# Layer 1's MLP products with the high and low parts of the activations as one 512-column operand, and layer 0's MLP in 256-column blocks with three matmuls

## The chip, the cores and the metric

The kernel runs on one core of a Trainium2 chip. The metric is the time of one execution in device microseconds (us). The engines are TensorE (PE: matmuls, and the weight loads PEld in front of them), VectorE (DVE), ScalarE (ACT), GpSimd (POOL) and SyncE (SP), which issues the weight DMAs.

## The reference

Two layers over 256 tokens with a model width of 2048 and a hidden width of 8192. The mixer (three kinds of token mixing between one input and one output projection) is not touched. The part that matters is the MLP of each layer, in fp32:

```python
mod = (cond @ ada_w[layer] + ada_b[layer])[:, None, :]
sh_a, sc_a, g_a, sh_m, sc_m, g_m = jnp.split(mod, N_MOD, axis=-1)
...
x = x + g_a * hybrid_mixer(...)
h = rmsnorm(x, norm_mlp_w[layer]) * (1.0 + sc_m) + sh_m
x = x + g_m * (jnp.square(jax.nn.relu(h @ w_ff1[layer])) @ w_ff2[layer])
...
return rmsnorm(x, final_norm_w)
```

## The kernel before

Activations lie transposed: 16 tiles of 128 features (k = 0 to 15) by T = 256 tokens. Every fp32 operand is split into a high part (rounded to fp32r) and a low part (what is left), and each product is three matmuls into the same sum: high weights by low activations, low weights by high activations, high by high. In `mm_b` (L252 to L254) the weights are the stationary 128x128 tile and the 256 token columns stream, four output tiles n to one k. In `mm_a` (L263 to L265), used for some input projections, the activations are stationary and 512 weight columns stream.

Weights arrive as `raw` pieces of 512 KB (2 k by 512 columns), six buffers. `split` makes of each the high part `wh` on ACT (L221, 128x1024) and the low part `wl` (L227) on DVE or, for the share `pool_share` of the pieces, on POOL; both have three buffers. A piece feeds 24 matmuls of `mm_b` (2 k, 4 n, three each). The share is 0.8 in layer 0's MLP and 0 in layer 1's.

In the MLP, `ff1` makes a block of 512 hidden features (16 k), and squares its ReLU into a high and a low tile of 128x1024 each (`square`: ACT L964 ReLU out of PSUM, L969 square, L971 high, DVE L972 low). There are 16 such blocks. `ff2` takes two of them (a step s) and adds to the residual X, in four output blocks nb of 512 features; the residual update is four DVE instructions of 128x256 per block, out of PSUM (`residual`, L796). Sums lie in two PSUM pairs `pj` of 1024 columns; the next block but one needs the pair again. Layer 1 does ff1 in one group of 16 k, layer 0 does its first 6 blocks in two groups of 8 k.

The normalised activations h are made by `h_make` in pairs of k: X times R (DVE L492), scale and shift (ACT L497, twice), high part (ACT L499), low part (DVE L500). R is the norm's factor: a sum of squares `ss` (DVE L374, L375), summed over features on PE (L383), DVE's Newton steps, and back over PE and ACT (L401, R copied by ACT L405). To have work for PE meanwhile, `lead` starts the next stage's first block on unnormalised activations (258 columns, L471 to L473; its operand is made ahead by `lead_u`, DVE L437 with L432 and L433, called by `early` out of the stage before), and `lead_out` puts R in afterwards (ACT L484, DVE L485). At the end of the program `ff2_tail` does the last 512 output features in four cuts of 128 (L1012 to L1014, residual L1017), with the sums of squares between.

The adaptive scale and shift vectors (`ada`, DVE L283, weights on their own DMAs) are computed piecemeal between these steps until the middle of layer 1. The order on each engine isn't written by hand: a scheduler at build time orders the instructions of every engine, so that an edit moves others.

Of the kernel before, what the change touches and what calls it, by code (L numbers as in the profile page):

```python
# [62 lines left out]
class Trunk:  # L63
# [166 lines left out]
    def chunk(self, src, nk, ncol=512):  # L230
# [11 lines left out]
        return out  # L242

# [204 lines left out]
    def lead(self, l, js, jc, wsrc, kts, stat_at):  # L448
# [5 lines left out]
        for c, k0 in enumerate(range(kts[0], kts[-1] + 1, 4)):  # L454
# [5 lines left out]
            w = self.chunk(wsrc(k0, nk), nk)  # L460
            if js == 3:
                self.step(nk / 4)
            for k in range(k0, k0 + nk):
                if k not in self.U:
                    self.lead_u(l, js, jc, [k, k + 1])
                (wh, wl), (uh, ul) = w[k - k0], self.U.pop(k)
                f, e = k == kts[0], k == kts[-1]
                for n in range(4):
                    s = slice(n * P, n * P + P)
                    o = ps[n][:, :LT]  # L470
                    nc.tensor.matmul(o, lhsT=wh[:, s], rhs=ul, start=f, stop=False)  # L471
                    nc.tensor.matmul(o, lhsT=wl[:, s], rhs=uh, start=False, stop=False)
                    nc.tensor.matmul(o, lhsT=wh[:, s], rhs=uh, start=False, stop=e)  # L473
# [4 lines left out]
        return ps  # L478

# [8 lines left out]
    def h_make(self, l, js, jc, kts, psum=False):  # L488
        nc = self.nc
        for k in kts[::2]:  # L490
# [8 lines left out]
            nc.scalar.copy(self.hh[:, k:k + 2, :], t)  # L499
            nc.vector.tensor_tensor(self.hl[:, k:k + 2, :], t, self.hh[:, k:k + 2, :].bitcast(F32), ALU.subtract)  # L500

    def hact(self, k):
        return self.hh[:, k, :], self.hl[:, k, :]
# [330 lines left out]
    def layer(self, l):  # L834
# [6 lines left out]
        for g, kts in enumerate(G):  # L841
            self.pump_until(l, 0, kts[-1])
            led = g == 0 and cfg["lead_win"]
            if led:
                ps = self.lead(l, 0, 1, lambda k, n: io["w_in"][l, 0, k // 4][:, k % 4:k % 4 + n, :], kts, cfg["stat_win"])
# [62 lines left out]
        for g, kts in enumerate(G):  # L908
# [4 lines left out]
            if led:  # L913
                ps = self.lead(l, 3, 4, lambda k, n: io["w_ff1"][l, 0, k // 4][:, k % 4:k % 4 + n, :], kts, cfg["stat_ff1"])
            self.h_make(l, 3, 4, kts)
            if led:
                acc[0] = self.slot()
                if kts[-1] == KT - 1:
                    self.lead_out(ps, acc[0], AF.Relu)
                    acc[0] = self.square(acc[0])  # L920
                else:
                    self.lead_out(ps, acc[0])
# [15 lines left out]
    def ff1(self, l, b, kts, acc=None):  # L938
        nc = self.nc
        ps = self.pair()  # L940
        for k0 in range(kts[0], kts[-1] + 1, 4):
            nk = min(4, kts[-1] + 1 - k0)
            r0 = k0 % 4
            w = self.chunk(self.io["w_ff1"][l, b, k0 // 4][:, r0:r0 + nk, :], nk)
            for i in range(nk):
                k = k0 + i
                self.mm_b(ps, w[i], self.hact(k), k == kts[0], k == kts[-1])
            self.step(nk / 4)
        if kts[-1] != KT - 1:
            if acc is None:  # L950
                acc = self.slot()
                nc.scalar.copy(self.flat(acc), ps)
            else:
                d = self.flat(acc)
                nc.vector.tensor_tensor(d, ps, d, ALU.add)
            return acc
        if acc is not None:
            t = acc
            d = self.flat(t)
            nc.vector.tensor_tensor(d, ps, d, ALU.add)  # L960
            nc.scalar.activation(t, t, AF.Relu)
        else:
            t = self.slot()
            nc.scalar.activation(self.flat(t), ps, AF.Relu)  # L964
        return self.square(t)

    def square(self, t):
        nc = self.nc
        nc.scalar.activation(t, t, AF.Square)  # L969
# [178 lines left out]
```

## Time and profile before

| | before |
|---|---|
| time of the runs | 2549.27 us median of 3 (2548.29 to 2551.44) |
| profiled execution | 2549.75 us, span of its trace 2548.0 us, mean granted TensorE clock 0.977 of full speed |
| PE busy | 2450.1 us (96% of the span) |
| DVE, ACT, POOL busy | 1583.2, 1180.9, 758.9 us |
| DMA | 630.45 MB, 247 GB/s over the span |

The profiled execution took 1.7 us more than its span, and 0.5 us more than the median of the runs. The stages in the trace: layer 0's MLP lies at about 540 to 1310 us, layer 1's at about 1800 to the end. PE is busy nearly throughout, so the trace is read for how far apart its matmuls stand and for the few places where it waits.

### The profile page before, as it was taken

Reading aid. Unit: us, or ns where it says so; the run is one execution under the profiler, and the core shown is the slowest. Engines: PE = TensorE matmul, PEld = TensorE weight load, DVE = VectorE, ACT = ScalarE, POOL = GpSimd, SP = SyncE. Lnnn points to the kernel's source line nnn. Section 1 sums busy time; section 2 is a strip of 40 time slices with the busy share of each in tenths; the row PEclk is TensorE's granted clock in tenths of the full one; section 3 lists DMA queues with packets and bytes.
Section 4 is the critical chain, followed back from the end, with each engine's and each line's share of the span. In section 5 each row is a group of like instructions: output and inputs, shape, how many; then the busy total and the mean of one; then the engine's idle time right before and its main releaser. Section 6 shows DMA issues by size and latency. Waiting matters only on the chain.

```text
span 2548.0 us, 46455 instructions
## 1 busy us (share of the span) xinstructions
PE 2450.1 (96%) x19016; PEld 2378.3 (93%) x19016; DVE 1583.2 (62%) x2427; ACT 1180.9 (46%) x1442; POOL 758.9 (30%) x314
## 2 busy tenths in 40 slices
PE   7999998979999999999989999999999999999997
PEld 6899977979999999999988989899999999999997
DVE  5867878788655444444478777656754555555554
ACT  4444455535544444444446446454644444344443
POOL 4786531212676766767650000000000000000000
PEclk8999999989999999999989999999999999999998
DMA  9899867788998888888867777555555555555552
GB/s 359 299 327 329 305 217 265 285 299 338 322 334 310 279 288 297 287 280 298 285 213 241 272 247 266 192 166 178 178 182 186 188 182 183 187 185 183 186 187 91
DMA packets 177246, 630.45 MB, mean 247 GB/s; under 512 B 19588, under 2 KB 24326, under 8 KB 177032
## 3 DMA queue, kind: packets, MB, share of 16 engines
q1 hardware_dynamic: 176600, 627.08, 70.8%
q8 instruction: 149, 2.44, 0.4%
q14 instruction: 65, 0.53, 0.1%
q10 hardware_dynamic: 432, 0.39, 0.1%
HBM read 625.30 MB, written 2.10 MB: 246 GB/s over the span
## 4 chain that ended last, share of the span: by engine, by line
PE 79%; DVE 9%; DMA 4%; issue 3%; POOL 3%; ACT 2%; SPq 0%; DVEq 0%; POOLq 0%; ACTq 0%
PE pj L253 23%; PE pj L252 23%; PE pj L254 23%; DMA ada<-ada_w 3%; POOL wl L227 3%; DVE ada L283 2%; PE pj L264 2%; PE pj L265 2%; PE pj L263 2%; DVE wl L227 2%; PE mx L620 1%; ACT wh L221 1%; DVE cv L709 1%; DVE blk L437 0%; DMA raw<-ada_w 0%
## 5 line engine op out<-in xcount | busy, mean ns | idle before, releaser
L221 ACT CAST wh<-raw 128x1024 fp32r<-128x1024 f32 x804 | 840.4, 1047 | 1129.8 <-PE pj L254 881.3
L227 POOL TENSOR_TENSOR wl<-raw,wh 128x1024 fp32r<-128x1024 f32 (+1 forms) x309 | 756.3, 2451 | 583.4 <-ACT wh L221 565.3
L227 DVE TENSOR_TENSOR wl<-raw,wh 128x1024 fp32r<-128x1024 f32 x495 | 615.7, 1246 | 487.4 <-ACT wh L221 486.7
L252 PE MATMUL pj<-hl,wh 128*128 128x256 f32 x2912 | 830.9, 286 | 9.5 <-DVE hl L500 8.2
L253 PE MATMUL pj<-hh,wl 128*128 128x256 f32 x2912 | 830.4, 285 | 7.2 <-DVE wl L227 7.2
L254 PE MATMUL pj<-hh,wh 128*128 128x256 f32 x2912 | 828.1, 284 | 0.0
L253 PE MATMUL pj<-blk,wl 128*128 128x256 f32 x2528 | 713.6, 282 | 6.6 <-DVE wl L227 5.2
L252 PE MATMUL pj<-blk,wh 128*128 128x256 f32 x2528 | 712.8, 282 | 2.8 <-ACT blk L538 1.5
L254 PE MATMUL pj<-blk,wh 128*128 128x256 f32 x2528 | 711.3, 281 | 0.0
L283 DVE SCALAR_TENSOR_TENSOR ada<-ada,cond 128x1024 f32<-128x1024 f32 x380 | 456.7, 1214 | 227.7 <-DMA ada<-ada_w 225.6
L252 PEld LDWEIGHTS pj<-hl,wh 128*128 128x128 f32 x2912 | 561.8, 193 | 10.7 <-DVE hl L500 8.9
L253 PEld LDWEIGHTS pj<-hh,wl 128*128 128x128 f32 x2912 | 562.4, 193 | 9.3 <-DVE wl L227 8.7
L254 PEld LDWEIGHTS pj<-hh,wh 128*128 128x128 f32 x2912 | 562.1, 193 | 0.2
L253 PEld LDWEIGHTS pj<-blk,wl 128*128 128x128 f32 x2528 | 478.5, 189 | 7.3 <-DVE wl L227 5.6
L252 PEld LDWEIGHTS pj<-blk,wh 128*128 128x128 f32 x2528 | 478.8, 190 | 3.4 <-ACT blk L538 1.9
L254 PEld LDWEIGHTS pj<-blk,wh 128*128 128x128 f32 x2528 | 479.3, 190 | 0.0
L1045 POOL TENSOR_TENSOR blk<-blk,R 128x1024 f32<-128x1024 f32 x1 | 2.4, 2357 | 1199.1 <-ACT R L405 1199.1
L264 PE MATMUL pj<-wl,hh 128*128 128x512 f32 x384 | 155.4, 405 | 8.5 <-DVE wl L227 8.4
L796 DVE SCALAR_TENSOR_TENSOR X<-pj,mod,X 128x256 f32<-128x256 f32 x284 | 117.8, 477 | 64.0 <-PE pj L254 63.9
L263 PE MATMUL pj<-wh,hl 128*128 128x512 f32 x384 | 153.2, 399 | 1.2 <-ACT wh L221 1.2
L265 PE MATMUL pj<-wh,hh 128*128 128x512 f32 x384 | 152.9, 398 | 0.0
L264 PEld LDWEIGHTS pj<-wl,hh 128*128 128x128 f32 x384 | 73.7, 192 | 24.5 <-DVE wl L227 10.7
(232 smaller groups left out, 1648.0 us busy)
## 6 DMA issues: line engine op xcount, KB each, us to landing
raw<-w_ff SPq DMA_DIRECT2D x508, 512.0 KB, 4.1
ada<-ada_w SPq DMA_DIRECT2D x380, 512.0 KB, 6.3
raw<-w_in SPq DMA_DIRECT2D x224, 512.0 KB, 5.0
raw<-w_out SPq DMA_DIRECT2D x64, 512.0 KB, 4.4
X<-x SPq DMA_DIRECT2D x4, 512.0 KB, 6.2
raw<-ada_w SPq DMA_DIRECT2D x4, 512.0 KB, 10.0
raw<-w_ff SPq DMA_DIRECT2D x8, 256.0 KB, 3.4
out<-blk SPq DMA_DIRECT2D x4, 512.0 KB, 2.8
```

The lines of the kernel that those rows point to most:

```text
L221: nc.scalar.copy(hi, raw)
L227: eng.tensor_tensor(lo, raw, hi.bitcast(F32), ALU.subtract)
L252: nc.tensor.matmul(o, lhsT=wh[:, s], rhs=al, start=st, stop=False, skip_group_check=True)
L253: nc.tensor.matmul(o, lhsT=wl[:, s], rhs=ah, start=False, stop=False, skip_group_check=True)
L254: nc.tensor.matmul(o, lhsT=wh[:, s], rhs=ah, start=False, stop=last, skip_group_check=True)
L263: nc.tensor.matmul(o, lhsT=al[:, s], rhs=wh, start=first, stop=False)
L264: nc.tensor.matmul(o, lhsT=ah[:, s], rhs=wl, start=False, stop=False)
L265: nc.tensor.matmul(o, lhsT=ah[:, s], rhs=wh, start=False, stop=last)
L283: nc.vector.scalar_tensor_tensor(raw, raw, 1.0, self.cond, ALU.mult, ALU.mult, accum_out=self.part[l][:, i, h:h + 1])
L620: nc.tensor.matmul(ps[:, i * P:i * P + P], lhsT=lt, rhs=v[:, j, c:c + P], start=first, stop=last, skip_group_check=True)
L709: V.scalar_tensor_tensor(y[:, s:], x[:, n, :T - s], w[:, 3 - s:4 - s], y[:, s:], ALU.mult, ALU.add)
L796: V.scalar_tensor_tensor(self.X(k), ps[:, n * T:n * T + T], self.mod[l][:, c:c + 1], self.X(k), ALU.mult, ALU.add)
```

## The change

One tile `h` holds high and low parts side by side for each k, and so do the tiles of squared activations. The weights w_ff1 and w_ff2 are laid out in blocks of 256 columns, so that a `raw` piece is 4 k by 256 columns (`chunk2`), of the same size as before. In layer 1 (`wide=True`) a product is two matmuls (`mm_w`): the high weights by the 512 columns [high | low], into a whole PSUM bank, and the low weights by the 256 high columns, into the bank's first half. In layer 0 it is still three matmuls of 256 columns (`mm_n`), and its pairs still hold 512 output features. A pair of layer 1 holds only 256, and each output has two sums to be added: in ff1 by an ACT copy and a DVE add, in ff2 by a second residual update. ReLU and square become one DVE instruction where the sum lies in SBUF, and the high and low tiles are made in halves. In the last ff2, `early` is called at the last two of eight output blocks. The piece of the diff that carries this (the change of layout on the host, `lead`'s weight lookup and the tail's slices follow from it):

```diff
+    def chunk2(self, src):
+        raw = self.raw.tile([P, 4, 256], F32, tag="raw", name=self.name("raw"))
+        self.wdma.append(self.nc.sync.dma_start(raw, src))
+        hi, lo = self.split(raw, 4, 256)
+        return [(hi[:, i, :], lo[:, i, :]) for i in range(4)]
+    def mm_w(self, ps, w, act, first, last):
+        nc = self.nc
+        wh, wl = w
+        for n in range(2):
+            s = slice(n * P, n * P + P)
+            o = ps[:, n * 512:n * 512 + 512]
+            nc.tensor.matmul(o.rearrange("p (a b) -> p a b", b=T), lhsT=wh[:, s], rhs=act, start=first, stop=False,
+                             skip_group_check=True)
+            nc.tensor.matmul(o[:, :T], lhsT=wl[:, s], rhs=act[:, 0, :], start=False, stop=last, skip_group_check=True)
+    def mm_n(self, ps, w, act, first, last):
+        nc = self.nc
+        wh, wl = w
+        for n in range(2):
+            s = slice(n * P, n * P + P)
+            o = ps[:, n * T:n * T + T]
+            for i, (a, b) in enumerate(((wh, 1), (wl, 0), (wh, 0))):
+                nc.tensor.matmul(o, lhsT=a[:, s], rhs=act[:, b, :], start=first and n == 0 and i == 0,
+                                 stop=last and i == 2, skip_group_check=True)
...
     def ff1(self, l, b, kts, acc=None):
+        wide = CFG[l]["wide"]
+        ps = None if wide else self.pair()
+        for h in range(2):
+            half = self.pair() if wide else ps[:, 512 * h:512 * h + 512]
+            for k0 in range(kts[0], kts[-1] + 1, 4):
+                w = self.chunk2(self.io["w_ff1"][l, 2 * b + h, k0 // 4])
+                for k in range(k0, k0 + 4):
+                    (self.mm_w if wide else self.mm_n)(half, w[k - k0], self.h[:, k], k == kts[0], k == kts[-1])
+                self.step(0.5)
+            if wide:
+                d = t[:, 2 * h:2 * h + 2, :]
+                p0, p1 = self.sums(half)
+                if fresh:
+                    nc.scalar.copy(d, p1)
+                else:
+                    nc.vector.tensor_tensor(d, p1, d, ALU.add)
+                nc.vector.tensor_tensor(d, p0, d, ALU.add)
...
     def square(self, t, relu=True):
+        if relu:
+            nc.vector.scalar_tensor_tensor(t, t, 0.0, t, ALU.max, ALU.mult)
+        else:
+            nc.scalar.activation(t, t, AF.Square)
+        out = []
+        for h in range(2):
+            s = self.slot((P, 2, 2, T), F32R)
+            nc.scalar.copy(s[:, 0], t[:, 2 * h:2 * h + 2, :])
+            nc.vector.tensor_tensor(s[:, 1], t[:, 2 * h:2 * h + 2, :], s[:, 0].bitcast(F32), ALU.subtract)
+            out.append(s)
...
     def ff2(self, l, s, hid, last):
+        for nb in range(6 if tail else 8):
+            if last and nb >= 6:
+                self.early(CFG[l + 1]["early_win"], nb - 6, l + 1, 0, 1)
+            if wide or nb % 2 == 0:
+                pair = self.pair()
+            ps = pair if wide else pair[:, nb % 2 * 512:nb % 2 * 512 + 512]
             for c in range(2):
+                w = self.chunk2(self.io["w_ff2"][l, nb, 2 * s + c])
                 for i in range(4):
+                    (self.mm_w if wide else self.mm_n)(ps, w[i], hid[c](i), c == 0 and i == 0, c == 1 and i == 3)
+                self.step(0.5)
+            for n in range(2):
+                k = 2 * nb + n
+                g = self.mod[l][:, 5 * KT + k:5 * KT + k + 1]
+                for c in range(n * 512, n * 512 + 512, T) if wide else (n * T,):
+                    V.scalar_tensor_tensor(self.X(k), ps[:, c:c + T], g, self.X(k), ALU.mult, ALU.add)
```

By the order of the instructions, L258 and L260 (`mm_w`) stand 1952 times each in the changed program. How the order moves is shown at three places. The first is layer 1's step from the lead to ff1's block 1. On PE before, with pj_19133 the last of the lead and pj_19468 block 1:

```order
L473 MATMUL pj_19133<-blk_19126,wh_19349 128x258
L252 MATMUL pj_19468<-hl,wh_19471 128x256
L253 MATMUL pj_19468<-hh,wl_19472 128x256
L254 MATMUL pj_19468<-hh,wh_19471 128x256
L252 MATMUL pj_19468<-hl,wh_19471 128x256
L253 MATMUL pj_19468<-hh,wl_19472 128x256
L254 MATMUL pj_19468<-hh,wh_19471 128x256
```

On PE now, where pj_19158 is the lead, pj_19496 the first half of block 1 (256 output columns), pj_19587 its second half, wh_19499 holds k 0 to 3 for the first half, wh_19543 k 8 to 11, and wh_19590 k 0 to 3 for the second half:

```order
L508 MATMUL pj_19158<-blk_19151,wh_19374 128x258
L258 MATMUL pj_19496<-h,wh_19499 128x512
L260 MATMUL pj_19496<-h,wl_19500 128x256
...
L258 MATMUL pj_19496<-h,wh_19543 128x512
L260 MATMUL pj_19496<-h,wl_19544 128x256
L258 MATMUL pj_19587<-h,wh_19590 128x512
L260 MATMUL pj_19587<-h,wl_19591 128x256
...
L260 MATMUL pj_19587<-h,wl_19591 128x256
L258 MATMUL pj_19496<-h,wh_19543 128x512
L260 MATMUL pj_19496<-h,wl_19544 128x256
```

A k takes two pairs of matmuls instead of four times three, and the second half's first piece is put into the middle of the first half's third. On DVE at the same place before, from the low part of the third pair of k (ht_19413) to that of the fifth (ht_19425):

```order
L500 TENSOR_TENSOR hl<-ht_19413,hh 128x512
L485 TENSOR_TENSOR blk_19449<-pj_19133,R 128x256
L227 TENSOR_TENSOR wl_19538<-raw_19535,wh_19537 128x1024
L492 TENSOR_TENSOR ht_19425<-X_93,R 128x512
L227 TENSOR_TENSOR wl_19592<-raw_19589,wh_19591 128x1024
L500 TENSOR_TENSOR hl<-ht_19419,hh 128x512
L492 TENSOR_TENSOR ht_19431<-X_93,R 128x512
L227 TENSOR_TENSOR wl_19598<-raw_19595,wh_19597 128x1024
L972 TENSOR_TENSOR blk_19465<-blk_19449,blk_19464 128x1024
L500 TENSOR_TENSOR hl<-ht_19425,hh 128x512
```

On DVE now, for the same three pairs (ht_19438, ht_19444, ht_19450):

```order
L548 TENSOR_TENSOR h<-ht_19438,h 128x2x256
L226 TENSOR_TENSOR wl_19566<-raw_19563,wh_19565 128x1024
L539 TENSOR_TENSOR ht_19450<-X_93,R 128x512
L532 TENSOR_TENSOR blk_19474<-pj_19158,R 128x256
L548 TENSOR_TENSOR h<-ht_19444,h 128x2x256
L539 TENSOR_TENSOR ht_19456<-X_93,R 128x512
L1020 SCALAR_TENSOR_TENSOR blk_19474<-blk_19474 128x1024
L548 TENSOR_TENSOR h<-ht_19450,h 128x2x256
```

Of the weight subtractions between the third and the fifth pair, one of three is left; L1020 stands where L972 stood. The second place is DVE at the boundary of the layers, from the last residual update of layer 0 (X_94) to the last sum of squares (L375), before:

```order
L796 SCALAR_TENSOR_TENSOR X_94<-pj_14018,mod_126,X_94 128x256 x4
L432 CAST blk_14201<-mod_127 128x2x2
L432 CAST blk_14208<-mod_127 128x2x2
L433 TENSOR_TENSOR blk_14201<-mod_127,blk_14201 128x2x2
L433 TENSOR_TENSOR blk_14208<-mod_127,blk_14208 128x2x2
L283 SCALAR_TENSOR_TENSOR ada_14907,part_125<-ada_14907,cond 128x1024
L374 TENSOR_TENSOR ss<-ss,blk_14197 128x512
L437 SCALAR_TENSOR_TENSOR blk_14201<-X_94,mod_127,blk_14201 128x256 x2
L437 SCALAR_TENSOR_TENSOR blk_14208<-X_94,mod_127,blk_14208 128x256
L283 SCALAR_TENSOR_TENSOR ada_14910,part_125<-ada_14910,cond 128x1024
L437 SCALAR_TENSOR_TENSOR blk_14208<-X_94,mod_127,blk_14208 128x256
L375 TENSOR_TENSOR ss<-ss,blk_14197 128x512
```

On DVE now, where L1052 is the residual, L467, L468 and L472 are the old L432, L433 and L437, and L409 and L410 are the old L374 and L375:

```order
L1052 SCALAR_TENSOR_TENSOR X_94<-pj_14085,mod_125,X_94 128x256 x2
L467 CAST blk_14226<-mod_126 128x2x2
L467 CAST blk_14233<-mod_126 128x2x2
L468 TENSOR_TENSOR blk_14226<-mod_126,blk_14226 128x2x2
L468 TENSOR_TENSOR blk_14233<-mod_126,blk_14233 128x2x2
L409 TENSOR_TENSOR ss<-ss,blk_14222 128x512
L472 SCALAR_TENSOR_TENSOR blk_14226<-X_94,mod_126,blk_14226 128x256
L410 TENSOR_TENSOR ss<-ss,blk_14222 128x512
L472 SCALAR_TENSOR_TENSOR blk_14226<-X_94,mod_126,blk_14226 128x256
L472 SCALAR_TENSOR_TENSOR blk_14233<-X_94,mod_126,blk_14233 128x256
L318 SCALAR_TENSOR_TENSOR ada_14932,part_124<-ada_14932,cond 128x1024
L472 SCALAR_TENSOR_TENSOR blk_14233<-X_94,mod_126,blk_14233 128x256
```

Both L283 ahead of L375 and three of the four L437 instructions have moved behind it, and two residual updates have moved ahead of the last block's end. On PE, 82 matmuls of layer 1's lead stand between the last matmul of layer 0's MLP and L383 before, and 57 now. The third place is DVE at the end of the program, where mx_27090 and mx_25410 are the first cut of the tail, before:

```order
L227 TENSOR_TENSOR wl_27139<-raw_27135,wh_27138 128x1024
L796 SCALAR_TENSOR_TENSOR X_93<-pj_26956,mod_127,X_93 128x256 x4
L227 TENSOR_TENSOR wl_27177<-raw_27173,wh_27176 128x1024
L1017 SCALAR_TENSOR_TENSOR X_94<-mx_27090,mod_127,X_94 128x256
L374 TENSOR_TENSOR ss<-ss,blk_27081 128x512
L375 TENSOR_TENSOR ss<-ss,blk_27081 128x512
```

On DVE now, where wl_25535 is the weight subtraction of the fourth cut:

```order
L226 TENSOR_TENSOR wl_25459<-raw_25455,wh_25458 128x1024
L1052 SCALAR_TENSOR_TENSOR X_93<-pj_25355,mod_126,X_93 128x256 x3
L226 TENSOR_TENSOR wl_25497<-raw_25493,wh_25496 128x1024
L1052 SCALAR_TENSOR_TENSOR X_93<-pj_25355,mod_126,X_93 128x256
L1080 SCALAR_TENSOR_TENSOR X_94<-mx_25410,mod_126,X_94 128x256
L226 TENSOR_TENSOR wl_25535<-raw_25531,wh_25534 128x1024
L409 TENSOR_TENSOR ss<-ss,blk_25404 128x512
L410 TENSOR_TENSOR ss<-ss,blk_25404 128x512
```

The fourth cut's subtraction now stands ahead of the sums of squares; before, wl_27177 was that of the third cut, and the fourth's came later.

## Rows read from the trace of the kernel before

**Rows 1.** The page's busy times, and the shares of the chain that ended last.

```profile
PE 2450.1 (96%) x19016; PEld 2378.3 (93%) x19016; DVE 1583.2 (62%) x2427; ACT 1180.9 (46%) x1442; POOL 758.9 (30%) x314
...
PE 79%; DVE 9%; DMA 4%; issue 3%; POOL 3%; ACT 2%; SPq 0%; DVEq 0%; POOLq 0%; ACTq 0%
```

**Rows 2.** Windows: us, PE, PEld, DVE, ACT, POOL busy, clock, DMA share, GB/s.

```profile
1826.00:2512.00 686.00, 685.19 (x5756) 685.19 (x5757) 363.91 (x385) 302.20 (x303) 0.00 (x0) 1.00 0.55 182
```

**Rows 3.** Timeline of ACT there: start, duration, [idle before, its releaser].

```profile
1901.79 1.05 ACT L221 CAST wh<-raw 128x1024 fp32r<-128x1024 f32 x1 [1.80 <-PE pj L254]
1904.63 1.05 ACT L221 CAST wh<-raw 128x1024 fp32r<-128x1024 f32 x1 [1.79 <-PE pj L254]
```

**Rows 4.** Timeline of PE in layer 1's input projections, with 512 columns.

```profile
1626.10 0.40 PE L263 MATMUL pj<-wh,hl 128*128 128x512 f32 x1
...
1629.97 0.39 PE L265 MATMUL pj<-wh,hh 128*128 128x512 f32 x1
```

**Rows 5.** Groups by line there: count | busy us, mean ns | idle before.

```profile
L227 DVE TENSOR_TENSOR wl<-raw,wh 128x1024 fp32r<-128x1024 f32 x240 | 293.8, 1224 | 305.6 <-ACT wh L221 305.5
...
L221 ACT CAST wh<-raw 128x1024 fp32r<-128x1024 f32 x240 | 251.5, 1048 | 353.9 <-PE pj L254 339.1 <-DVE wl L227 14.2 <-ACT wh L221 0.7
...
L796 DVE SCALAR_TENSOR_TENSOR X<-pj,mod,X 128x256 f32<-128x256 f32 x120 | 49.8, 478 | 15.9 <-PE pj L254 15.9
```

**Rows 6.** Timeline, layer 1's activations being made and first used.

```profile
1813.36 0.28 PE L252 MATMUL pj<-hl,wh 128*128 128x256 f32 x1
...
1816.87 0.68 DVE L500 TENSOR_TENSOR hl<-ht,hh 128x512 fp32r<-128x512 f32 x1
...
1821.54 0.69 DVE L500 TENSOR_TENSOR hl<-ht,hh 128x512 fp32r<-128x512 f32 x1
...
1826.07 0.69 DVE L500 TENSOR_TENSOR hl<-ht,hh 128x512 fp32r<-128x512 f32 x1
...
1826.81 0.39 PE L252 MATMUL pj<-hl,wh 128*128 128x256 f32 x1 [1.41 <-DVE hl L500]
```

**Rows 7.** Timeline of DVE, POOL and PE at the boundary of the layers.

```profile
1307.12 1.66 DVE L796 SCALAR_TENSOR_TENSOR X<-pj,mod,X 128x256 f32<-128x256 f32 x4 [3.53 <-PE pj L254]
1308.69 2.10 DVE L432 CAST blk<-mod 128x4 fp32r<-128x4 f32 x2
...
1312.30 1.22 DVE L283 SCALAR_TENSOR_TENSOR ada<-ada,cond 128x1024 f32<-128x1024 f32 x1 [1.31 <-DMA ada<-ada_w]
...
1312.48 7.69 POOL L227 TENSOR_TENSOR wl<-raw,wh 128x1024 fp32r<-128x1024 f32 x3 [1.79 <-ACT wh L221]
...
1313.44 2.00 DVE L374 TENSOR_TENSOR ss<-ss,blk 128x512 f32<-128x512 f32 x1
1315.36 5.48 DVE L437 SCALAR_TENSOR_TENSOR blk<-X,mod,blk 128x256 fp32r<-128x256 f32 x3
...
1322.31 0.68 DVE L375 TENSOR_TENSOR ss<-ss,blk 128x512 f32<-128x512 f32 x1
...
1323.04 1.87 PE L383 MATMUL pj<-ones,ss 128*128 128x1 f32 x8 [6.12 <-DVE ss L375]
```

**Rows 8.** Windows behind that wait, columns as in rows 2.

```profile
1323.00:1331.00 8.00, 7.96 (x40) 7.96 (x41) 6.85 (x18) 1.04 (x1) 0.00 (x0) 0.56 0.67 239
1331.00:1340.00 9.00, 9.00 (x77) 9.00 (x77) 2.05 (x7) 4.24 (x8) 5.20 (x3) 1.00 0.46 142
```

**Rows 9.** Timeline of PE's waits in layer 0's lead.

```profile
551.26 1.35 PE L383 MATMUL pj<-ones,ss 128*128 128x1 f32 x8 [2.00 <-DVE ss L375]
...
566.75 1.01 PE L293 MATMUL mx<-part,fold 128*128 128x4 f32 x4 [5.20 <-DVE blk L485]
```

**Rows 10.** Timeline of PE and DVE at the end of the program.

```profile
2516.69 0.69 DVE L375 TENSOR_TENSOR ss<-ss,blk 128x512 f32<-128x512 f32 x1
...
2517.44 1.44 PE L383 MATMUL mx<-ones,ss 128*128 128x1 f32 x8 [1.91 <-DVE ss L375]
...
2518.17 1.22 DVE L227 TENSOR_TENSOR wl<-raw,wh 128x1024 fp32r<-128x1024 f32 x1 [0.79 <-ACT wh L221]
```

More of the change, by code (lines that the diff above doesn't have):

```diff
@@ L478, in lead, with lead_win, get, lead_ff1 @@
         return ps
+    def lead_win(self, l):
+        def get(k, nk):
+            w = self.chunk(self.io["w_in"][l, 0, k // 4][:, k % 4:k % 4 + nk, :], nk)
+            return lambda i, n: tuple(x[:, n * P:n * P + P] for x in w[i])
+        return get
+    def lead_ff1(self, l):
+        def get(k, nk):
+            w = [self.chunk2(self.io["w_ff1"][l, b, k // 4]) for b in range(2)]
+            return lambda i, n: tuple(x[:, n % 2 * P:n % 2 * P + P] for x in w[n // 2][i])
+        return get
     def lead_out(self, ps, dst, func=AF.Identity, scale=1.0):
@@ L844, in layer @@
             if led:
[L845 removed]
+                ps = self.lead(l, 0, 1, self.lead_win(l), kts, cfg["stat_win"])
             if l > 0:
@@ L957, in ff1 @@
[L957 to L961, printed above, removed]
-        else:
[L963 to L969, printed above, removed]
-        hi, lo = self.slot(dt=F32R), self.slot(dt=F32R)
-        nc.scalar.copy(hi, t)
-        nc.vector.tensor_tensor(lo, t, hi.bitcast(F32), ALU.subtract)
-        return hi, lo
+        done = kts[-1] == KT - 1
@@ new lines, in ff1 @@
+        fresh = acc is None
+        t = self.slot() if fresh else acc
+        wide = CFG[l]["wide"]
[15 more added lines that the diff above has]
+                nc.vector.tensor_tensor(d, p0, d, ALU.add)
@@ new lines, in ff1, with square @@
+        if not wide:
+            d = self.flat(t)
+            if not fresh:
+                nc.vector.tensor_tensor(d, ps, d, ALU.add)
+            elif not done:
+                nc.scalar.copy(d, ps)
+            else:
+                nc.scalar.activation(d, ps, AF.Relu)
+        return self.square(t, wide or not fresh) if done else t
+    def square(self, t, relu=True):
+        nc = self.nc
+        if relu:
+            nc.vector.scalar_tensor_tensor(t, t, 0.0, t, ALU.max, ALU.mult)
+        else:
+            nc.scalar.activation(t, t, AF.Square)
[5 more added lines that the diff above has]
+            out.append(s)
+        return lambda i: out[i // 2][:, :, i % 2, :]
@@ L978, in ff2 @@
         tail = last and l == DEPTH - 1
[L979 to L980 removed]
+        wide = CFG[l]["wide"]
+        for nb in range(6 if tail else 8):
[4 more added lines that the diff above has]
+            ps = pair if wide else pair[:, nb % 2 * 512:nb % 2 * 512 + 512]
             for c in range(2):
[L982 to L985 removed]
+                w = self.chunk2(self.io["w_ff2"][l, nb, 2 * s + c])
                 for i in range(4):
[L987 to L992 removed]
+                    (self.mm_w if wide else self.mm_n)(ps, w[i], hid[c](i), c == 0 and i == 0, c == 1 and i == 3)
[5 more added lines that the diff above has]
+                    V.scalar_tensor_tensor(self.X(k), ps[:, c:c + T], g, self.X(k), ALU.mult, ALU.add)
+            if last and nb % 2 == 1:
+                self.stat_piece(nb // 2)
+                if nb == 7:
                     self.early(CFG[l + 1]["early_win"], 2, l + 1, 0, 1)
             if tail:
[L995 to L996 removed]
+                for n in range(2):
+                    self.final_scale(2 * nb + n)
         if tail:
```

83 lines of the change are left out of this document (28 added, 55 removed).

## The prediction

> **What bounds the kernel now.** I start with the page's busy times and the chain that ended last. TensorE is busy 96% of the span, and its own instructions make 79% of that chain [rows 1]; most of the time is the time of matmuls issued one behind another. Then I cut out layer 1's MLP by windows: in 686 us TensorE is idle for 0.8 us, at clock 1.00, while VectorE is busy 363.9 us, ScalarE 302.2, GpSimd nothing and the DMA engines 55% [rows 2]. There the spacing of matmuls alone is the time. The groups say the same from the other side: VectorE's weight subtractions waited 305.5 us for ScalarE's casts, and the casts 339.1 us for TensorE to give buffers back [rows 5]. So both run ahead and are held up by TensorE, not the reverse.
>
> The spacing can be read without the modelled ends. Two casts of weight pieces start 2.84 us apart, and a piece feeds 24 matmuls: 118.3 ns each [rows 3]. Over the whole stretch, 240 casts [rows 5] make 686 / (240 x 24) = 119.1 ns [rows 2]. For 512 streamed columns the timeline of the input projections gives 17 steps between 1626.10 and 1629.97: 227.6 ns each [rows 4]; its starts are rounded to 0.01 us and neighbours of it vary, so I take 227 to 229.
>
> **The change part by part.** *The pair of matmuls.* A 512-column and a 256-column matmul replace three of 256 columns, so one spacing of 512 stands for two of 256. That saves 2 x 118.3 - 229 = 7.6 ns to 2 x 119.1 - 227 = 11.2 ns; in the middle 2 x 118.6 - 227.6 = 9.6 ns. Columns streamed are the same, 768; what goes is the part of a spacing that doesn't grow with columns. Pairs: 15 blocks of ff1 x 4 x 16 k = 960, and 62 blocks of ff2 x 2 x 8 k = 992, together 1952, the count in the order. The term is -18.7 us, between -14.8 and -21.9. Layer 0 keeps 256 columns and its number of matmuls: nothing there.
>
> The trace has no 512-column matmul alternating with a 256-column one, so this rests on each keeping its own spacing. The Trainium skill, "TensorE: Matmul & The Clock Gate", section "Back-to-back issue gap", gives 262 cycles for 256 columns and 518 for 512 at full clock, which would save only 6 cycles or 2.5 ns a pair, an estimate of 4.9 us in all. The rows stand about 10 ns above these figures at both widths, and I go by the rows; what the rule would make of the kernel is a rival below.
>
> *Evacuation and squaring in layer 1.* A pair of PSUM is free again when VectorE has read it. ff2 takes 124 more residual instructions of 0.415 us (four in 1.66 [rows 7]): 51 us. In ff1 each of 15 blocks takes two adds of 128x512 and one max-multiply of 128x1024; priced as the subtraction of that size, 1.22 us [rows 5], that is 2.45 us a block, 37 us. VectorE comes to 364 + 51 + 37 = 452 of some 667 us. ScalarE loses a square and exchanges a ReLU for a copy. The cover is TensorE's work on the other pair: an ff2 block lasts 16 pairs x 345.9 ns = 5.5 us, in which VectorE has two subtractions and four residuals, 2.4 + 1.7 = 4.1 us. I cost it at nothing; without that cover it is up to 1.7 us a block.
>
> *Layer 1's lead to block 1.* The first half-block needs a k every 2 x 345.9 = 692 ns instead of 12 x 118.6 = 1423, but the activations are made no faster. Before, TensorE starts on them at 1813.36, and the low parts of the third, fourth and fifth pair of k are ready 0.69 us after 1816.87, 1821.54 and 1826.07 [rows 6]. At those times the new pace would wait 1.4, 3.3 and 3.1 us at the three (each pair of k feeds 1.38 us of work), 7.9 in all. In the new order, two of three weight subtractions there are gone, and the second half-block's first piece covers the sixth pair and the next. Replaying that order with the durations of the rows I get waits of 1.5, 2.1, 1.2 and 0.5 us, 5.3; before it was 1.41 [rows 6]. Term: +3.9, between -1.4 (all waits gone) and +6.5.
>
> *Layer 0's lead.* TensorE waits 2.00 us for the sum of squares and 5.20 us for the lead's result to be taken out [rows 9]. The half-blocks want activations sooner, for eight k instead of sixteen (at most half of 6.5, +3.2), while the take-out stands some 2 us earlier in the new order (-2). I take +0.5.
>
> *The boundary of the layers.* TensorE waits 6.12 us for the last sum of squares, although the last residual starts at 1307.12 and that sum only at 1322.31 [rows 7]. Between them VectorE runs an `ada` instruction that waited 1.31 us for its DMA, and three lead operands that take 5.48 us, 1.83 each where a residual update of the same size takes 0.48 [rows 5], while GpSimd is at work beside it for 7.69 us [rows 7]. After the wait the clock is at 0.56 for 8 us, in which 40 matmuls run; at 1.00 there are 77 in 9 us [rows 8]. 40 would take 4.7, so 3.3 us go there. In the new order two residual updates, casts of 2.10 us, two small ones of 0.24, two sums and one lead operand follow the last matmul: 0.8 + 2.1 + 0.2 + 0.7 + 0.5 + 0.7 = 5.0 us; if sums and operand are slowed as L374 and L437 there (2.00, 1.83, 2.00 [rows 7]), 9.0. TensorE has 57 lead matmuls ahead of L383, 57 x 0.119 = 6.8 us. So it waits between nothing and 2.2 us, plus newly late reads; I take 1.3, which saves 4.8, and 2.7 of the clock's 3.3. Term: -7.5. The bounds are 0 (something else is late, say the square on ScalarE or a weight piece on GpSimd) and -9.4 (no wait, full clock).
>
> *The end.* The second sum of squares now follows the subtraction of the tail's fourth cut. That one started at 2518.17 against 2516.69 for the sum [rows 10]: one duration of 1.22 behind it and one more sum (0.69) is +3.4 at most. ScalarE's cast for it may come earlier now, so I take +2.0, from 0.
>
> Sum: -18.7 + 3.9 + 0.5 - 7.5 + 2.0 = -19.8. The profiled execution took 2549.75 us, 1.75 more than its span of 2548.0; that gives 2529.95. The median of the runs is 0.48 lower: **2529.5 us**.
>
> **The rivals.**
> - *Only the matmuls get cheaper.* The boundary's 7.5 us aren't saved, since another instruction is late at L383. For it: a scheduler that does not know of slow reads beside GpSimd ordered both. Against: the instructions that filled the time are gone from before the sum. 2529.5 + 7.5 = 2537.
> - *The small saving.* A pair costs 2.5 ns less than three, by whatever adds to the wide matmul when its neighbour has other weights: 1952 x 2.5 = 4.9 us instead of 18.7, 2543. This is the result of the skill's two figures; rows 3 and 4 speak against it.
> - *Weight loads set the 256-column spacing.* TensorE's loads are busy as long as its matmuls [rows 2]. If columns alone cost (227.6 - 118.3) / 256 = 0.427 ns each, 768 take 328 ns, 27 less than three spacings: 52 us, 2496. Against: then 512 columns should show 218.6 and not 227.6.
> - *VectorE takes the bound* (the other side). Now 62 blocks of ff2 and 30 halves of ff1 must each be read out before the pair is wanted again, and weight subtractions queue behind the reads. If each of the 92 costs TensorE 0.35 us, that is +32: 2561. It decides from 25 / 92 = 0.28 us a block, and starts when VectorE's 4.1 us in 5.5 become more than 5.5, or when the read waits behind a subtraction that itself waits for a cast. Against it: the 305 us that those subtractions wait now [rows 5].
> - *No saving*, a 512-column matmul costing two of 256 here: 2548.
>
> **How the numbers follow.** A measurement of this kernel can tell about 0.2% from no change, 5.1 us: faster is below 2544.2, slower above 2554.4. My forecast has 70%, with a range of its own of 2521 to 2538 (the bounds of the terms don't all fall on one side). Only the matmuls: 15%. The small saving 4%, weight loads 4%, VectorE 5%, no saving 2%. Faster: 70 + 15 + 4 and half of the small saving's 4, less a point for the first two at their upper ends: 90%. Slower: VectorE's 5%. The same: the rest, 5%. The range for 8 in 10 takes the forecast and most of the second case: 2520 to 2541.
>
> **What would show it.** In layer 1's MLP, 16 pairs between casts should take 5.53 us for two weight pieces, and the stretch some 667 us at clock 1.00 with TensorE's idle time still about 1 us; VectorE some 452 us busy. A pair of 353 ns means the small saving, of 328 the weight loads; TensorE waiting on L1052 or L226 in every block means VectorE. At layer 1's block 1 waits of some 5 us on L548; at the boundary a wait at L418 below 3 us with the clock hardly falling; at the end a wait of 3 to 5 us at L418. I am wrong if the spacing of a wide matmul beside a narrow one is its own, or if a re-ordered stage I costed at nothing (layer 1's mixers, layer 0's steady blocks) has a new wait of more than 5 us.

## The result, and the profile after

The changed kernel takes 2607.73 us (median of 4 runs, 2605.78 to 2608.13) against 2548.78 for the kernel before: ratio 1.0229, interval 1.0217 to 1.0241. It is 59 us slower; 2529.5 was forecast.

The page of the changed kernel, whose lines answer to [rows 1]:

```profile
PE 2450.5 (94%) x17064; PEld 2283.1 (88%) x17064; DVE 1707.2 (66%) x2635; ACT 1160.6 (45%) x1461; POOL 752.8 (29%) x314
...
PE 72%; DVE 10%; issue 6%; POOL 6%; DMA 5%; ACT 1%; SPq 0%; DVEq 0%; POOLq 0%; ACTq 0%
```

TensorE's own share of the chain fell from 79% to 72%: other engines' work ends last more often. The waits of TensorE over the whole span, longest sums first (us in total, times, longest), name it:

```profile
PE pj L270 <- DVE X L1052: 47.0, 31, 4.4
PE pj L270 <- ACT wh L220: 12.8, 11, 1.2
```

L270 is `mm_n`, the three-matmul form of layer 0, and L1052 the residual update of ff2. To see in which stage the time went, I take the start of the four sum-of-squares matmuls (L383, now L418) as marks. From layer 0's to layer 1's it was 771.8 us before and is 835.6 now, 63.8 more; to layer 1's second 473.6 and 477.6; to the one at the end 720.8 and 712.1, 8.7 less. The whole loss and more is in layer 0's MLP, where the prediction put +0.5 us for the lead, -7.5 for the boundary and nothing for the steady blocks. Windows over 600 to 1290 us (us, then busy PE, PEld, DVE, ACT, POOL, clock, DMA share, GB/s), first of the kernel before:

```profile
600.00:1290.00 690.00, 690.00 (x5791) 690.00 (x5790) 349.13 (x515) 303.90 (x298) 460.11 (x187) 1.00 0.86 302
```

and of the changed kernel:

```profile
600.00:1290.00 690.00, 642.28 (x5239) 635.90 (x5238) 346.48 (x484) 266.88 (x276) 414.92 (x170) 0.98 0.78 275
```

TensorE went from no idle time to 48 us of it in the same stretch, with VectorE no busier. A timeline around one such wait (start, duration, instruction, and in brackets the idle time before it and its releaser):

```profile
721.65 0.88 DVE L1052 SCALAR_TENSOR_TENSOR X<-pj,mod,X 128x256 f32<-128x256 f32 x2 [2.36 <-PE pj L270]
...
722.67 0.36 PE L270 MATMUL pj<-blk,wh 128*128 128x256 f32 x1 [1.06 <-DVE X L1052]
```

VectorE starts as soon as TensorE has finished the first half of the pair, and TensorE starts the second half only when VectorE is through. The next half, which opens another pair, comes without a wait: the waits stand some 12.6 us apart, two halves. The order of the changed program on PE, with the semaphores that each waits for, shows it without any time. In the first row pj_8871 gets the last matmul of its first half, in the third the first of its second half, and pj_9008 is the pair after it:

```
L270 MATMUL pj_8871<-blk_7290,wh_8910 128x256
L270 MATMUL pj_9008<-blk_7140,wh_9011 128x256 [waits Activation_49]
L270 MATMUL pj_8871<-blk_7140,wh_8942 128x256 [waits DVE_49]
```

The third row writes the pair's second bank, while VectorE reads the first, and yet it waits for VectorE. The middle row is a matmul of the next pair that the scheduler put in front; it waits for a cast, 1.1 to 1.2 us at a time, which is the second line of the waits above.

At a new step the wait is longer. VectorE, GpSimd and TensorE there, from the timeline:

```profile
852.85 7.51 POOL L226 TENSOR_TENSOR wl<-raw,wh 128x1024 fp32r<-128x1024 f32 x3 [4.22 <-ACT wh L220]
...
855.93 4.97 DVE L1027 TENSOR_TENSOR blk<-blk,blk 128x512 fp32r<-128x512 f32 x2
860.83 0.86 DVE L1052 SCALAR_TENSOR_TENSOR X<-pj,mod,X 128x256 f32<-128x256 f32 x2
...
861.75 0.58 PE L270 MATMUL pj<-blk,wh 128*128 128x256 f32 x1 [3.79 <-DVE X L1052]
```

and the window behind it:

```profile
861.70:865.50 3.80, 3.75 (x18) 3.75 (x19) 2.05 (x3) 0.00 (x0) 0.00 (x0) 0.51 0.79 322
```

The residual stands behind two low-part subtractions of the next hidden tile, which take 2.23 and 2.82 us while GpSimd works beside them. TensorE then runs 3.8 us at its lower clock (granted 0.51). The Trainium skill, "SBUF — State Buffer", section "SBUF: two separate sides", says that a VectorE instruction with two SBUF inputs and a GpSimd instruction that reads SBUF hold a shared pair of ports exclusively, the loser blocking fully. The trace agrees: the two take about as long as one of the three GpSimd subtractions (2.38 to 2.77 us), against 0.69 for the same size where GpSimd is idle [rows 6].

### The profile page after: what moved, and what is told of

Read it like the earlier page. It is cut to its first block, busy times and chain, and to the rows that moved or that the text cites. A ratio compares the mean times of both kernels' runs of the same rounds, so it can differ in the third digit from the quotient of the medians.

```text
span 2606.3 us, 42813 instructions
## 1 busy us (share of the span) xinstructions
PE 2450.5 (94%) x17064; PEld 2283.1 (88%) x17064; DVE 1707.2 (66%) x2635; ACT 1160.6 (45%) x1461; POOL 752.8 (29%) x314
## 4 chain that ended last, share of the span: by engine, by line
PE 72%; DVE 10%; issue 6%; POOL 6%; DMA 5%; ACT 1%; SPq 0%; DVEq 0%; POOLq 0%; ACTq 0%
PE pj L270 19%; PE pj L258 17%; PE pj L260 9%; POOL wl L226 6%; PE pj L288 5%; PE pj L287 5%; PE pj L289 5%; DMA ada<-ada_w 4%; DVE ada L318 2%; PE pj L299 2%; PE pj L300 2%; PE pj L298 2%; DVE wl L226 2%; DVE blk L472 1%; DVE X L1052 1%
## 5 line engine op out<-in xcount | busy, mean ns | idle before, releaser
L270 PE MATMUL pj<-blk,wh 128*128 128x256 f32 x2048 | 388.5, 289 | 57.9 <-DVE X L1052 47.0
L270 PEld LDWEIGHTS pj<-blk,wh 128*128 128x128 f32 x2048 | 329.2, 195 | 65.5 <-issue 26.3
L270 PE MATMUL pj<-h,wh 128*128 128x256 f32 x1984 | 361.0, 284 | 3.2 <-ACT wh L220 2.2
L258 PE MATMUL pj<-blk,wh 128*128 128x512 f32 x992 | 347.9, 394 | 0.0
L258 PE MATMUL pj<-h,wh 128*128 128x512 f32 x960 | 337.6, 396 | 3.1 <-DVE h L548 3.0
L270 PEld LDWEIGHTS pj<-h,wh 128*128 128x128 f32 x1984 | 311.1, 192 | 3.8 <-ACT wh L220 2.6
L270 PE MATMUL pj<-blk,wl 128*128 128x256 f32 x1024 | 293.7, 287 | 0.0
L287 PE MATMUL pj<-h,wh 128*128 128x256 f32 x960 | 276.3, 288 | 8.1 <-DVE h L548 6.8
L270 PE MATMUL pj<-h,wl 128*128 128x256 f32 x992 | 282.1, 284 | 0.3 <-DVE wl L226 0.3
L288 PE MATMUL pj<-h,wl 128*128 128x256 f32 x960 | 275.9, 287 | 5.7 <-DVE wl L226 5.7
L260 PE MATMUL pj<-blk,wl 128*128 128x256 f32 x992 | 278.4, 281 | 0.0
L289 PE MATMUL pj<-h,wh 128*128 128x256 f32 x960 | 273.9, 285 | 0.0
L260 PE MATMUL pj<-h,wl 128*128 128x256 f32 x960 | 269.0, 280 | 0.0
L1052 DVE SCALAR_TENSOR_TENSOR X<-pj,mod,X 128x256 f32<-128x256 f32 x376 | 169.8, 479 | 146.1 <-PE pj L270 112.3
L258 PEld LDWEIGHTS pj<-blk,wh 128*128 128x128 f32 x992 | 186.3, 188 | 43.7
L258 PEld LDWEIGHTS pj<-h,wh 128*128 128x128 f32 x960 | 180.1, 188 | 47.1 <-DVE h L548 4.0
L270 PEld LDWEIGHTS pj<-blk,wl 128*128 128x128 f32 x1024 | 200.3, 196 | 0.0
```

What stands on the lines that cost most here:

```text
L258: nc.tensor.matmul(o.rearrange("p (a b) -> p a b", b=T), lhsT=wh[:, s], rhs=act, start=first, stop=False, skip_group_check=True)
L260: nc.tensor.matmul(o[:, :T], lhsT=wl[:, s], rhs=act[:, 0, :], start=False, stop=last, skip_group_check=True)
L270: nc.tensor.matmul(o, lhsT=a[:, s], rhs=act[:, b, :], start=first and n == 0 and i == 0, stop=last and i == 2, skip_group_check=True)
L287: nc.tensor.matmul(o, lhsT=wh[:, s], rhs=al, start=st, stop=False, skip_group_check=True)
L288: nc.tensor.matmul(o, lhsT=wl[:, s], rhs=ah, start=False, stop=False, skip_group_check=True)
L289: nc.tensor.matmul(o, lhsT=wh[:, s], rhs=ah, start=False, stop=last, skip_group_check=True)
```

## The experiments

Each kernel's time is a median of the runs it got, with the ratio to the kernel before on the same chip (2548.5 to 2548.7 there).

**Reading the pair once (e1_read_once).** In layer 0 all four residual updates of a pair are made after its second half:

```diff
-            for n in range(2):
-                k = 2 * nb + n
+            for n in range(2) if wide else range(0 if nb % 2 else 4, 4):
+                k = 2 * nb + n if wide else 2 * nb - 2 + n
...
-                    V.scalar_tensor_tensor(self.X(k), ps[:, c:c + T], g, self.X(k), ALU.mult, ALU.add)
+                    V.scalar_tensor_tensor(self.X(k), (ps if wide else pair)[:, c:c + T], g, self.X(k), ALU.mult, ALU.add)
```

> Layer 0's ff2 makes its residual updates for both halves of a PSUM pair together, after the second half, as the kernel before did; all else is the changed kernel. Theory A (the second half of a pair waits until VectorE has read the first half, because both lie in one pair): the 47.0 us of waits for L1052 in layer 0 go, the 12.8 us of waits for casts beside them, and the lower clock; layer 0's MLP, 835.6 us from its sum of squares to layer 1's, comes back to 765 to 775, and the time to about 2541 us (2536 to 2547). Theory B (VectorE is too late with the residual, wherever it is read, because weight pieces and ada queue before it): the four updates together are later still, the waits move to the next pair but one, and the time stays above 2580 us. Theory C (blocks of 256 columns cost TensorE by themselves, in weight order or clock): above 2570 us without a wait to show.

2535.47 us, ratio 0.9958 (0.9945 to 0.9972). No wait for L1052 is left in layer 0, TensorE is busy 690.00 of 690 us between 600 and 1290, and the first stage is 766.7 us:

```profile
600.00:1290.00 690.00, 690.00 (x5797) 689.89 (x5796) 377.34 (x551) 294.21 (x304) 458.61 (x188) 1.00 0.85 301
```

Theory A holds, half a microsecond below its range; B and C fall. Against the changed kernel this is 72 us less.

**A pair for each half (e2_own_pair).** The read stays where the change put it:

```diff
-            if wide or nb % 2 == 0:
-                pair = self.pair()
-            ps = pair if wide else pair[:, nb % 2 * 512:nb % 2 * 512 + 512]
+            pair = self.pair()
+            ps = pair if wide else pair[:, 0:512]
```

> Layer 0's ff2 gives each half its own PSUM pair (of which half is unused) and reads it at the same point as the changed kernel. Theory A (a shared pair): no wait any more, since the pair is wanted again only 5.7 us later; 2541 us (2536 to 2549). Theory B (VectorE late): the waits of 1.06 us go, since 5.7 us are enough for them, but those of 2.3 to 4.4 us, where ada and weight pieces stand before the read, mostly stay: some 2555 us. Theory C: above 2570 us.

2532.55 us, ratio 0.9943 (0.9931 to 0.9955); windows over the same stretch:

```profile
600.00:1290.00 690.00, 688.25 (x5765) 687.86 (x5765) 381.79 (x533) 291.53 (x299) 455.53 (x187) 1.00 0.85 300
```

The waits of 2.3 to 4.4 us are gone as well as those of 1.06, though VectorE has as many instructions as before (2635) and reads at the same point. So VectorE was late only for a matmul that follows at once; with one more half of 5.7 us between, it is in time. It is the sharing, together with reading in halves, that cost the time. The kernel is 3 us below theory A's range; the boundary of the layers is shorter too (below). It is faster than both kernels of the case, than the one before by 16 us.

**The wait doubled (e9_shared_both).** The changed kernel with layer 1 in the three-matmul form too (`wide=False`), so that its ff2 shares pairs as well:

> The changed kernel with three matmuls of 256 columns in layer 1 too, so that two output blocks share a pair there as well and each is read when it is done: the suspected wait is doubled. Theory A (the shared pair): layer 1's ff2 gets 31 waits for L1052 of about 1.1 us each, the floor that layer 0 shows, with no ada and no GpSimd there to lengthen them, and about 36 us of time; with layer 0's loss of some 66 us 2540.7 + 66 + 36 = 2643 us. Theory B (VectorE's other work makes the residual late): layer 1, where VectorE has no ada left after its middle, shows no waits and the time is some 2607 us.

2658.93 us, ratio 1.0438 (1.0401 to 1.0476). The waits of TensorE in layer 1's MLP, and one of them:

```profile
PE pj L270 <- DVE X L1052: 25.5, 24, 1.1
PE pj L270 <- ACT wh L220: 7.9, 7, 1.1
```

```profile
2069.28 0.88 DVE L1052 SCALAR_TENSOR_TENSOR X<-pj,mod,X 128x256 f32<-128x256 f32 x2 [0.54 <-PE pj L270]
...
2070.31 0.36 PE L270 MATMUL pj<-blk,wh 128*128 128x256 f32 x1 [1.06 <-DVE X L1052]
```

31 waits, as counted beforehand, all at the floor of about 1.1 us: 24 put down to the read, 7 to the cast for a matmul put ahead of it at the start of a step. Of the 1.06, 0.88 are the two reads. The time is 16 us above theory A's and 52 above theory B's. About 8 of the 16 are in layer 0, whose loss is 74 us (832.0 to the boundary against 758.0 in e7_narrow_own below) and not 66. The rest is in layer 1, whose MLP is 43.6 us longer than in e7_narrow_own (769.6 against 726.0), not 36: with start-up each of the 24 gaps is 1.22 us, and the 7 are 1.3 and 0.4 more behind the matmul put ahead, together 41 us. The floor is what the shared pair costs when VectorE has nothing else to do; layer 0's extra comes from its queue and the clock.

**What the two-matmul form is worth.** First the kernel that reads once, with layer 1 narrow (`wide=False`, e3_narrow); its final scaling reads six of the sixteen output tiles before their last update:

> As the first kernel (read once), and layer 1 also with three matmuls of 256 columns in the new blocks. By the spacings of the changed kernel's trace (351.0 ns a pair against 357.2 for three) the two-matmul form is worth 1952 x 6.3 ns = 12.3 us, less 1.6 us more of waits at layer 1's lead: this kernel should be 9 to 13 us slower than the first, about 2551 us. If the narrow layout in layer 1 costs nothing else it lands within 5 us of the kernel before. Rival: with the prediction's 9.6 ns a pair it would be 17 to 19 us slower than the first.

2550.13 us, ratio 1.0011 (1.0001 to 1.0021): 14.7 us slower than e1_read_once, above the 9 to 13 expected and below the rival's 17 to 19. Then the same with a PSUM pair for each half (e7_narrow_own):

> As e2_own_pair, with three matmuls of 256 columns in layer 1 too, each half in its own pair. What the two-matmul form is worth in layer 1, with the same way of reading PSUM in both: by the spacings 12.3 us, less 1.6 of waits at layer 1's lead, so 2543 us (2541 to 2546); by the comparison of e3_narrow with e1_read_once 14.7 us, 2547 us; by the prediction's 9.6 ns a pair 2550 us.

2540.72 us, ratio 0.9969 (0.9955 to 0.9982), 8.2 us slower than e2_own_pair and just below the branch of the spacings. The two differences, 14.7 and 8.2, are no further apart than single runs of one kernel (2536 to 2545 for this one), but layer 1's MLP itself, mark to mark, is 726.8 and 726.0 us narrow against 712.2 and 712.1 wide, 14 to 15 us in both. In this narrow form the activations make TensorE wait 5.0 us at the lead, against 3.0 in the wide one.

**The spacing of the wide matmul.** In the changed kernel's trace, the mean start-to-start times in layer 1's MLP are 233.1 ns after a wide matmul and 117.5 after a narrow one; three rows of the timeline as an example:

```profile
2040.03 0.40 PE L258 MATMUL pj<-h,wh 128*128 128x512 f32 x1
2040.27 0.28 PE L260 MATMUL pj<-h,wl 128*128 128x256 f32 x1
2040.39 0.40 PE L258 MATMUL pj<-h,wh 128*128 128x512 f32 x1
```

Three kernels ask why it is 233 and not the 227.6 of [rows 4]. The order wide, wide, narrow, narrow (both `n` of the wide one first, e4_order):

> As the first kernel (read once), and layer 1's matmuls in the order wide, wide, narrow, narrow instead of wide, narrow, wide, narrow. If the 233 ns of a wide matmul (228 in the input projections) come from the narrow one in front of it, one in two wide ones falls to 228 and the pairs to about 348 ns on average: 1952 x 2.5 ns = 5 us less than the first, about 2536 us. If a wide matmul with its operand from the activations always takes 233, the same time as the first within 2 us.

2535.78 us, ratio 0.9952 (0.9938 to 0.9966), the same as e1_read_once, as the second branch said; a wide matmul takes 232.9 and 233.1 ns on average (ff2 and ff1), the same behind a wide one as behind a narrow one. Then e2_own_pair with contiguous operands (e5_flat):

```diff
-            nc.tensor.matmul(o.rearrange("p (a b) -> p a b", b=T), lhsT=wh[:, s], rhs=act, ...)
+            nc.tensor.matmul(o, lhsT=wh[:, s], rhs=act.rearrange("p a b -> p (a b)"), ...)
...
-            nc.scalar.copy(s[:, 0], t[:, 2 * h:2 * h + 2, :])
+            nc.scalar.copy(s[:, :, 0], t[:, 2 * h:2 * h + 2, :])
...
```

> As the kernel with a pair for each half (e2_own_pair), with the wide matmul's operand contiguous: high and low part of a squared tile lie next to each other for each k (as those of h do already), and operand and output are given as one run of 512 columns. If the wide matmul's 233 ns against 228 in the input projections come from its split operand or output, its spacing falls to about 228 and the time by up to 1952 x 5 ns = 10 us, to some 2523 us; the strided writes of the squared tiles may give a part back. If not, the spacing stays at 232 to 234 and the time within 2 us of e2_own_pair (2532.6).

2531.16 us, ratio 0.9921 (0.9903 to 0.9939), within 2 us of e2_own_pair as the second branch said, with 232.3 ns in ff2 and 233.6 in ff1. Then e2_own_pair with no narrow matmul in layer 1 at all (the low weights also by the low activations, whose product is added, e8_all_512):

```diff
-            nc.tensor.matmul(o[:, :T], lhsT=wl[:, s], rhs=act[:, 0, :], ...)
+            nc.tensor.matmul(o.rearrange("p (a b) -> p a b", b=T), lhsT=wl[:, s], rhs=act, ...)
```

> As e2_own_pair, with the narrow matmul of layer 1 made wide too (the low weights also by the low activations, which adds their product): 1952 times 512 columns instead of 256. It measures a row of 512-column matmuls with these operands and no narrow one between. If the 233 ns come from the alternation of widths, the spacing falls to 228; if from what these matmuls read or write, it stays at 232 to 234. Time up by 1952 x (228 to 234 less 118) = 215 to 226 us, some 2750 to 2760 us.

2744.3 us in one run, 6 us under the expected range. Now ff1's matmuls, with h, stand 226.8 ns apart, and ff2's, with the squared tiles, 232.5. So in ff1 the mixture of widths costs some 4 ns a pair: 226.8 and the 120.0 of narrow ones alone (e7_narrow_own) make 346.8, and the pair takes 350.8. In ff2 the wide matmul is dearer by itself: 232.5 and 118.2 make 350.7, and the pair takes 350.4. Each branch of the expectation is right for one half. Why the mixture costs anything isn't shown; that a wide matmul takes the same behind a wide one in e4_order speaks against the neighbour just in front. What the squared tiles have that h has not stays open too: it isn't the split operand.

**The two-matmul form in layer 0 as well** (`wide=True`, a pair for each half, e6_wide_both):

> As e2_own_pair, with the two-matmul form in layer 0 too: 992 + 1024 = 2016 pairs there. By the spacing measured in layer 1 (6.2 ns a pair) 12.5 us less, 2520 us, if VectorE keeps up. VectorE's work in layer 0's MLP rises from about 349 to 440 us of 690, with ada pieces among it and instructions that run longer beside GpSimd. Rival: reads of PSUM come late behind those, 96 blocks at 0.2 us or more of wait each eat the gain: 2533 us or above, with waits for L1052 and L1005 to be seen on TensorE.

2563.4 us, ratio 1.0057 (1.0041 to 1.0072): the rival holds. Waits of TensorE from 600 to 1350 us:

```profile
PE pj L258 <- DVE X L1051: 19.0, 9, 5.0
PE pj L418 <- DVE ss L410: 7.1, 1, 7.1
PE pj L506 <- DVE X L1051: 5.3, 1, 5.3
PE pj L258 <- DVE blk L1005: 3.2, 3, 2.0
```

VectorE is busy 463.46 of 690 us between 600 and 1290 and still late: ten waits for L1051 of up to 5.3 us, where reads stand behind `ada` and behind instructions that run longer beside GpSimd (two subtractions of 2.58 and 2.83 us ahead of the wait at 1239 us).

## Why the prediction was wrong, point by point

**The step that failed** is one sentence of the part on the pair of matmuls: "Layer 0 keeps 256 columns and its number of matmuls: nothing there." The number of matmuls was right. What it left out is where the residual stands: a pair of layer 0 still holds 512 output features, but it is now read in two halves, and the second half's matmuls wait for the first half's read. The prediction did price a late evacuation, for layer 1 alone, and took for its cover "TensorE's work on the other pair"; in layer 0 the work that follows is in the same pair, so there is no cover. Its last sentence did name a new wait in "layer 0's steady blocks" as a sign of being wrong, but neither the sum nor a rival gave that a price; the 5% for slower stood for VectorE in layer 1.

Measured: 75 us, from the changed kernel to the one with a pair for each half (72 to the one that reads once). Where they lie is told by the starts of TensorE's instructions from 600 us to the mark, lead and sums left out, counting what exceeds one spacing of 119 ns. In the changed kernel L270 waits for L1052 in 31 places, 53.1 us (the 47.0 above are idle time by modelled ends); matmuls that wait for casts, most of them put ahead of those, make 13.4 us (1.5 without the sharing); and small gaps make 17.2, of which 14.6 are matmuls at the lower clock (3.9 without). The kernel with a pair for each half waits 4.2 us there for low weight parts, which the changed one does not. That makes 53.1 + 11.9 + 13.3 - 4.2 = 74.1.

The wait is one that the program makes, and none of the data: the matmul writes another bank than the one that L1052 reads, the trace puts its release down to L1052, and with a pair for each half it is gone. The Trainium skill, "PSUM — Partial Sum Buffer", section "PSUM bank collisions raise a hardware error", says to guard by bank and quadrant, and that accesses to different banks run clean at the same time. By that rule the halves of a pair need no guard between them. Whether they could run without it was not tried; the experiments take the need away instead.

**What was right, and by how much.** Without the sharing the kernel takes 2532.55 us, 16.2 less than before, where the sum said 19.8.

| term | predicted us | measured us | from |
|---|---|---|---|
| pairs of matmuls in layer 1 | -18.7 | -12.2 | stage 712.1 less waits of 3.0 and 3.8, against 720.8 less 1.4 and 1.9 |
| evacuation and squares in layer 1 | 0 | 0 | TensorE busy 659.94 of 660, below |
| layer 1's lead | +3.9 | +1.6 | waits 3.0 against 1.4 |
| layer 0's lead | +0.5 | about 0 | waits 4.7 and 1.7, and new ones of 1.0 for h, against 5.2 and 2.0 [rows 9] |
| boundary | -7.5 | -7.1 | e1_read_once to e2_own_pair |
| end | +2.0 | +1.9 | wait 3.77 against 1.91 [rows 10] |
| layer 0's ff2 | 0 | +72 to +75 | e1_read_once, e2_own_pair |

Without layer 0's ff2 the measured terms add up to -15.8. That this is near the -16.2 is in part luck: the first two stages, added, are 1228.1 to 1234.8 us in three traces whose kernels differ in layer 1's MLP alone (e2_own_pair, e7_narrow_own, e8_all_512), so a term of a few us read from them is not told from scatter.

*The matmuls* were mis-sized by a third: 6.2 ns a pair of matmuls, not 9.6. Rows 3 and 4 are of other operands and of rows of one width, and each width did not keep its own spacing, which the prediction named as the condition of the term. The measured saving lies between the forecast and the 4.9 us of the rival *The small saving*. Against three narrow ones in the new blocks the form saves 14 us of the stage; the new blocks with narrow matmuls are some 2 us longer than the old, waits taken out, and 1.5 of that are 17 matmuls at the lower clock behind the waits at the lead.

*Evacuation in layer 1* was free, as forecast, with VectorE busy 440 us of 660 (forecast 452 of 667). Windows of the changed kernel, answering to [rows 2]:

```profile
1900.00:2560.00 660.00, 659.94 (x3767) 576.16 (x3766) 439.94 (x550) 282.76 (x303) 0.00 (x0) 1.00 0.62 188
```

and by groups, VectorE's subtractions still wait 187.1 us for casts, against 305.5 in [rows 5]:

```profile
L226 DVE TENSOR_TENSOR wl<-raw,wh 128x1024 fp32r<-128x1024 f32 x236 | 288.5, 1223 | 187.1 <-ACT wh L220 187.1
```

The rival "VectorE takes the bound" is wrong there. It is true of layer 0 in the two-matmul form (e6_wide_both), where VectorE's queue has `ada` in it and GpSimd beside it.

*Layer 1's lead*: three waits of 1.23, 0.99 and 0.79 us for h, at the third to fifth pair of k; the replay had 5.3 us with one more.

*The boundary*: the last sum is ready 5.1 us after the last residual starts, and L418 waits for nothing, in the timeline of the changed kernel, answering to [rows 7]:

```profile
1381.31 0.88 DVE L1052 SCALAR_TENSOR_TENSOR X<-pj,mod,X 128x256 f32<-128x256 f32 x2 [0.82 <-PE pj L270]
...
1385.75 0.68 DVE L410 TENSOR_TENSOR ss<-ss,blk 128x512 f32<-128x512 f32 x1
...
1387.73 0.95 PE L418 MATMUL pj<-ones,ss 128*128 128x1 f32 x8
```

The kernel that reads once has four residuals after the last matmul again, and the wait is back:

```profile
1317.75 1.87 PE L418 MATMUL pj<-ones,ss 128*128 128x1 f32 x8 [6.14 <-DVE ss L410]
```

Windows of 8 us from the mark, first of the kernel that reads once, then of the one with a pair for each half:

```profile
1317.70:1325.70 8.00, 7.95 (x39) 7.96 (x40) 6.85 (x18) 1.04 (x1) 0.00 (x0) 0.53 0.74 238
1314.40:1322.40 8.00, 8.00 (x70) 8.00 (x69) 8.00 (x12) 2.24 (x3) 6.00 (x3) 1.00 0.47 172
```

At the mark more was gained than forecast: the whole wait, where 1.3 us were to be left, and the clock stays at 1.00. Later waits, 5.2 us against 2.8 up to 1350 us, take a part of it back, and net the first stage loses 5.2 us and the second 1.9. So the early read that costs 75 us within the layer is worth some 7 at its end. The three lead operands that the prediction puts at 1.83 us each [rows 7] lasted 2.61, 2.56 and 0.47 us by the trace: 1.83 is their mean, and two of them stood beside GpSimd for about one of its subtractions each.

*The end*: the sum now follows the fourth cut's subtraction, as the order showed:

```profile
2574.80 1.22 DVE L226 TENSOR_TENSOR wl<-raw,wh 128x1024 fp32r<-128x1024 f32 x1 [0.64 <-ACT wh L220]
2575.95 0.68 DVE L409 TENSOR_TENSOR ss<-ss,blk 128x512 f32<-128x512 f32 x1
2576.67 0.69 DVE L410 TENSOR_TENSOR ss<-ss,blk 128x512 f32<-128x512 f32 x1
...
2577.41 1.05 PE L418 MATMUL mx<-ones,ss 128*128 128x1 f32 x8 [3.77 <-DVE ss L410]
```

## What to carry to other kernels

When a change cuts a block that lives in one buffer into parts that are read when each is done, look for the next writer of that buffer: if it is the next instruction of the bound engine, the reader's whole way (here 1.1 us for 0.88 of reading) is paid each time, and any work queued before the reader on top. It can be read beforehand from the order with its waits; a term "same number of instructions" says nothing of it. Give each part its own buffer, or read the whole once, and price a spacing only from rows with the same operands and the same neighbours.

## What the hardware showed that I had not expected

A 512-column matmul isn't of one price: 227.6 ns with weights streaming [rows 4], 226.8 with h, 232.5 with the squared tiles (both e8_all_512). With 256 columns it is the other way round, 120.0 with h and 118.2 with the squared tiles (e7_narrow_own). A wide and a narrow one with h take some 4 ns more together than each kind in rows of its own. The clock kept its full level through waits of 1.06 us every 12.6 us (granted 1.00 from 750 to 800 us of the changed kernel), and fell to 0.51 behind one of 3.79.
